# A different order for the S5 part of a hybrid backbone kernel: Toeplitz transfers, lag matrices, two sums and two pair steps

## The chip, the cores and the metric

The kernel runs on one core of one Trainium2 chip. A core has TensorE (PE in the profile; its weight loads are PEld), VectorE (DVE), ScalarE (ACT), GpSimd (POOL) and SyncE (SP, which here only issues DMAs). Time is device microseconds of one execution; lower is better.

## The reference, cut to what matters

With DEPTH = 1 the backbone is one layer: a bidirectional S5 mixer (64 groups of 16 channels, 64 complex states each) and a SwiGLU feed-forward part, both behind an RMS norm with a modulation (shift, scale, gate) that comes from the conditioning vector by one large matrix, `ada_w`. There are 1024 latent tokens of width 1024, and 256 context tokens that only feed the first state of each scan.

```python
m_l = jnp.split(sc @ ada_w[i] + ada_b[i], N_MOD, axis=-1)      # sc = silu(c), ada_w is 1024 x 6144
h_l = modulate(rms_norm(x, norm_mix[i]), m_l[0][:, None], m_l[1][:, None])
...
lam_bar = jnp.exp(lam * jnp.exp(log_step)[:, None])             # per direction
b_bar = ((lam_bar - 1.0) / lam)[..., None] * lax.complex(b_re, b_im)
bu = jnp.einsum('lgh,gnh->lgn', u, b_bar)
bu = bu.at[0].add(lam_bar * h0)                                 # h0: the context's last state
_, h = lax.associative_scan(_linear_combine, (a, bu), axis=0)
y = jnp.einsum('lgn,ghn->lgh', h, c_mat).real                   # forward plus backward
...
y = y.reshape(h.shape) + d_skip * h
g = jax.nn.gelu(y)
y_l = g * jax.nn.sigmoid(g @ w_glu + b_glu)
x = x + m_l[2][:, None] * y_l
h_l = modulate(rms_norm(x, norm_ffn[i]), m_l[3][:, None], m_l[4][:, None])
x = x + m_l[5][:, None] * swiglu(h_l, ffn_w1[i], ffn_w3[i], ffn_w2[i])
return rms_norm(x, norm_final)
```

## The kernel before, in words

The tokens are cut into chunks of 8. The scan runs over chunks only: 32 of the context, then 128 of the latents. What a token gets from tokens of its own chunk is a product with a Toeplitz matrix; what it gets from earlier chunks is the chunk's start state times factors. The 64 groups are worked in four quarters q of 16 groups (eight group pairs) and in 16 half-blocks `hb` (eight blocks of 8 groups, two directions).

*The first part* (a loop over `hb`) makes the chunk sums of each half-block on PE (`sums`), copies them to the state store `STQ` in SBUF, and joins neighbouring chunks there: `pair(hb, eng)` is four tensor-tensor instructions, on GpSimd for the half-blocks listed in `PPAIR` and on VectorE for the others; `pair(hb - 1, ...)` is issued in round `hb`, the last one, 15, behind the loop. The first tiles of the second part of `ada_w` are loaded here (`ADA2`).

*The scan* (`scan`) then runs on VectorE as one long chain of small instructions, with `fill_ops` between them. Meanwhile the other engines go through PROG1, a string of steps that `run` executes word by word. Each engine works its own share of these words in this order, so the string is at the same time the order of PE's, ACT's, POOL's and SP's queues. The steps that matter here:

- `A`n: modulation tiles up to number n (of 64). A tile is 128 x 512 of `ada_w`, 256 KB; `ada` multiplies it on PE (L534) into one PSUM bank `pm` and issues on SP, in `ada_load` (L523), each later tile whose buffer has been freed (`was`): tiles 42 to 45 reuse the buffers of 30 to 33, 46 to 49 those of 34 to 37, 50 to 53 those of 38 to 41, 54 to 57 those of 46 to 49, 58 to 61 those of 50 to 53, and 62 and 63 those of 54 and 55.
- `B`: the input factors are turned (L821). `O`: a PSUM bank is cleared on ACT for a `K` step.
- `C`qp: factors of quarter q, made on POOL by `cl_ops`. For each direction there are two products and a sum (parts 0 and 2, first half of the list), then a product and a sum (parts 1 and 3). `HOWS` says how each sum is made: `P` on PE with the unit matrix (four matmuls, L691) with two copies out by ACT (L692), `Y` by an accumulating DMA, `E` on POOL by one tensor-tensor instruction of 128 x 1024.
- `K`i: lag matrices of half a quarter (`k_mats`): many small matmuls (L839 to L847), two copies out on ACT and two DMAs that ACT issues to DRAM (L852). It needs both directions of the quarter's factors.
- `T`u: one Toeplitz transfer on SP (L860), 256 KB from DRAM to one of four buffers `KQ`; T0 to T3 need K0 and K1, T4 to T7 need K2 and K3, and so on.
- `L`, `G`, `q`: load of a quarter's output matrix (issued by ACT), its sign change on ACT (L669), its sum on POOL.
- `F`: a fill of a quarter's odd chunk states on POOL (eight instructions). F11 keeps temporaries where step R1 later writes.
- `R`i: the backward states of block i, turned by a copy on ACT (L954). `P`i: the block's output for the first half of the chunks on PE, a Toeplitz part (`x_mm`, L985, it needs T(2i) and T(2i+1)) and a state part (`states_mm`, L974, it needs R); `S` and `X` are the same two parts apart. `Y`: copies to SBUF on ACT (L1044).
- `M`: the finished modulation is copied (ACT), written to DRAM (SP, L933), transposed (PE, L937) and used.

After PROG1, PROG2 handles the second half of the chunks (`Z`, `N`, `D`), the GELU and the gated linear unit; `N0` is its first PE work. The feed-forward part follows, long streams of matmuls on PE.

PROG1 begins, before: `A22 G1 B0 A26 A30 C01 A34 A38 O0 C03 q1 A42 K0 A46 K1 L2 A50 C10 C11 A54 T0 T1 T2 T3 O2 C12 C13 G2 A58 K2 A64 K3 L3 F10 q2 C20 F11 R0 P0 ...`

Of the kernel before, what the change touches and what calls it, by code (L numbers as in the profile page):

```python
# [26 lines left out]
NS = 64  # L27
EPS = 1e-6
MAGIC = 12582912.0
HOWS = "YPYP EPEP PPPP EEEE"  # L30
ZEN = "VVSVSVSV"
PROG1 = ("A22 G1 B0 A26 A30 C01 A34 A38 O0 C03 q1 A42 K0 A46 K1 L2 A50 C10 C11 A54 T0 T1 T2 T3 O2 C12 C13 G2 A58 K2 A64 K3 L3 F10 q2 C20 F11 R0 P0 Y0 Y1 T4 T5 R1 P1 Y2 Y3 T6 T7 M0 M1 C22 G3 R2 P2 Y4 Y5 C21 R3 P3 Y6 Y7 C23 q3 K4 K5 T8 T9 T10 T11 C30 C31 C32 C33 R4 P4 Y8 Y9 R5 P5 Y10 Y11 O6 K7 K6 T12 T13 T14 T15 w0 l1 M2 m0 F31 w1 R6 S6 R7 S7 X6 Y12 Y13 X7 Y14 Y15")
PROG2 = ("Z0 N0 Z1 Z2 D0 Z3 N1 D1 Z4 H0 H1 N2 D2 Z5 H2 N3 D3 Z6 H3 N4 Z7 D4 H4 I0 J0 N5 D5 I1 J1 H5 W0 W1 N6 D6 I2 J2 H6 I3 J3 W2 W3 x0 x1 x2 x3 N7 D7 I4 J4 H7 V1 b0 w20 w21 l1 I5 J5 g03 g13 I6 J6 g23 g05 g15 I7 J7 V2 g26 x10 x11 x12 x13")
NS1, NS2 = 10, 1
LOG2E = 1.4426950408889634
# [7 lines left out]
def s5_ffn_kernel(tc, a, out):  # L43
    nc = tc.nc
    V, S, E, PE, SY = nc.vector, nc.scalar, nc.gpsimd, nc.tensor, nc.sync
    ctx = ExitStack()
    with ctx:
        ctx.enter_context(tc.manual_schedule())
        sb = ctx.enter_context(tc.tile_pool(name="sb", bufs=1))
        def region(tag, kb, dt=F32):  # L50
            return sb.tile([P, int(kb * 256)], dt, tag=tag, name=tag)
# [12 lines left out]
        R0 = region("r0", 7)  # L64
# [11 lines left out]
        def tt(o, x, y, op, eng=V):  # L76
            eng.tensor_tensor(out=o, in0=x, in1=y, op=op)  # L77
# [104 lines left out]
        def t_(i):  # L182
            return view(RA, 0.75 + 0.25 * i, [G])
# [11 lines left out]
        def ada1(h, *ks):  # L195
            for k in ks:
                for b in range(2):
                    i = 2 * b + h
                    PE.matmul(prow[32 * i:32 * i + 2], scs[:, k], stage[h][k][:, b], start=k == 0, stop=k == 7, tile_position=(0, 32 * i))
# [16 lines left out]
        k3, r1, pw2, be, al, rp, r2, u2, pw3, sn, q1, q2, tc_, td_ = [t_(i) for i in range(14)]  # L216
# [176 lines left out]
        def bd(hb):  # L393

            return divmod((0, 2, 1, 3)[hb] if hb < 4 else hb, 2)
# [63 lines left out]
        def mix_rows():  # L459
            S.copy(r4, prow.rearrange("p (m n) -> p m n", m=4))  # L460
# [38 lines left out]
        def u_act(b, n0, n1):  # L499
            for g in range(8 * b + n0, 8 * b + n1):  # L500
                S.activation(X[:, g], X[:, g], AF.Identity, bias=cols[:, 0, 0, g:g + 1], scale=cols[:, 0, 1, g:g + 1])
# [78 lines left out]
        def sums(hb):  # L580
            b, d = bd(hb)
            for j in range(2):
                w, pv = Win[hb % 3][:, j], pv2()
                for ri in range(2):
                    for i in range(4):
                        c0 = 160 * (i // 2)
                        PE.matmul(pv[64 * (i % 2):64 * (i % 2) + 64, ri, c0:c0 + 160], w[:, i, 64 * ri:64 * ri + 64],  # L587
                                  U[:, 8 * b + 4 * j + i], start=True, stop=True)
                pv = pv[:, :, 0:320].rearrange("p r (e c) -> p c r e", e=2)
                e = 8 * (b % 2) + 4 * d + 2 * j  # L590
                st = STQ[b // 2][:, :, :, e:e + 2]
                if d == 0:
                    S.copy(st, pv)
                else:
                    cp = V.tensor_copy if (hb, j) == (13, 1) else S.copy
                    cp(st[:, 159:31:-1], pv[:, 32:160])
                    cp(st[:, 31::-1], pv[:, 0:32])
# [10 lines left out]
        def rot(*args):  # L608
            for op in rot_ops(*args):
                op()  # L610

        def rots(*args):

            for a_ in args:
                rot(*a_, V, (LTb, lbt[:, 256:512]))
# [13 lines left out]
        def pair(hb, eng):  # L629
            b, d = bd(hb)  # L630
            e = 8 * (b % 2) + 4 * d
            st = STQ[b // 2][:, :, :, e:e + 4]
            a_ = (st[:, 33:96:2], st[:, 32:95:2], LQ[0] if eng is V else LS[:, 0], 16 * (b // 2) + e)
            if eng is V:
                rots(a_)
            else:
                rot(*a_, E, ptmp)
# [33 lines left out]
        def cs_sum(q):  # L671
            c0, c1, c2 = (Cs[q % 2][:, i].rearrange("p d g h -> p (d g h)") for i in range(3))
            tt(c2, c0, c1, SUB, E)
# [3 lines left out]
        def cl_ops(q, d):  # L677
# [5 lines left out]
            def prod(i, o):  # L683
                tt(o, bc(Cs[q % 2][:, (2, 1, 0)[i], d], 2, T), bc(fac[i][:, ::1 - 2 * d].rearrange("p t a -> p a t"), 3, HC), MUL, E)

            def add(o, how, last):
                if how == "P":
                    for h in range(2):
                        hs, pc = slice(4 * h, 4 * h + 4), pw([512])
                        for i, src in enumerate((o, ct)):  # L690
                            PE.matmul(pc, ident, src[:, hs].rearrange("p g t h -> p (g t h)"), start=i == 0, stop=i == 1)  # L691
                        S.activation(o[:, hs].rearrange("p g t h -> p (g t h)"), pc, AF.Copy, scale=-1.0 if last else 1.0)  # L692
                elif how == "Y":
                    E.dma_start(o, ct, accum_op=ADD)
                else:
                    tt(o, o, ct, SUB if last else ADD, E)

            h0, h1 = HOWS.split()[q][2 * d:2 * d + 2]
            return [lambda: prod(0, ct), lambda: prod(1, o0), lambda: add(o0, h0, False), lambda: prod(2, o1), lambda: add(o1, h1, True)]

        PPAIR = (3, 5, 7, 8, 9, 11, 12, 13, 15)
        UACT = {1: (2, 0, 4), 2: (2, 4, 8), 3: (3, 0, 4), 4: (3, 4, 8)}
        UACT.update({5 + i: (4 + i // 2, 4 * (i % 2), 4 * (i % 2) + 4) for i in range(8)})
        UCTX = {1: 2, 3: 3, 6: 4, 7: 5, 9: 6, 11: 7}
# [13 lines left out]
        for hb in range(16):  # L718
            sums(hb)
            ada1(1, *ADA1.get(hb, ()))  # L720
            if hb == 0:
                power8()
            if hb == 3:
                mix_rows()
            if hb >= 11 and hb in UACT:
                u_act(*UACT[hb])
            for n in BLTR.get(hb, (hb + 2,)):
                if n < 16:
                    bl_tr(n)
            if hb == 3:  # L730
                mix_turn()
            if hb == 4:
                mix_scale(1)
                mix_sel(1)
            if hb in RSL:
                rs_lat(RSL[hb])
            if hb == 4:
                mix_cols(1)
                tq = pA.tile([P, 512], F32, tag="r3", name="tq")
                LQ += [t[:, o_:o_ + 192].rearrange("p (r e) -> p r e", e=G) for t, o_ in ((tq, 0), (tq, 192), (LTb, 256))]  # L740
            if hb == 0:
                tt(Xc[:, 16:], ctxT[:, 16:], bc(rcp, 1, G - 16), MUL)
            if hb == 1:
                powers(0)
            if hb == 2:
                powers(1)
                SY.dma_start(BXY[:, 1], a["bxy"][:, 3])
                SY.dma_start(abr, a["abr"])
            if hb < 11 and hb in UACT:
                u_act(*UACT[hb])  # L750
            if hb in UCTX:
                u_ctx(UCTX[hb])
            if hb in (9, 10):
                bl_sum(hb + 5)
            if hb >= 1:
                pair(hb - 1, E if hb - 1 in PPAIR else V)
            if hb == 5:
                powers(2, 3)
            for a_ in CTREE.get(hb, ()):
                ctx_tree(*a_)  # L760
            if hb + 6 in (7, 9, 11, 12, 14, 15):
                lb_psum(hb + 6)
            if hb not in (9, 10):
                bl_sum(hb + 5)
            bl_make(hb + 6)
            if hb == 3:
                pw_mul(PW[:, 2:3], PW[:, 0:1], PW[:, 1])
                tt(KD.rearrange("p q g h -> p (q g) h"), bc(pat, 1, 8), bc(dcol, 2, HC), MUL, E)
            if hb == 4:
                pw_mul(PW[:, 4:6], PW[:, 0:2], PW[:, 3])  # L770
                pw_mul(PW[:, 6:7], PW[:, 2:3], PW[:, 3])
            if hb in (6, 8):
                pw_full(hb // 2 - 3)
            if hb == 6:
                cs_load(0)
            if hb == 8:
                cs_sign(0)
            if hb == 11:
                V.tensor_copy(LQ[4], SQ[4])
                cs_load(1)  # L780
            if hb == 12:
                cs_sum(0)
            for _ in range(CLAT.get(hb, 0)):
                CL0.pop(0)()
            ada_load(ADA2.get(hb, 0))
# [380 lines left out]

        run(PROG1)
        psW.__exit__(None, None, None)
# [160 lines left out]
        G2 = region("c3", 16, R32)  # L1329
# [503 lines left out]
```

## Time and profile before

| | us |
|---|---|
| median of 3 runs (lowest, highest) | 1036.97 (1035.01, 1037.14) |
| the profiled execution | 1037.25 |
| its span, first to last instruction | 1035.40 |
| busy in the span: PE, PEld, DVE | 972.2, 757.4, 782.9 |
| busy in the span: ACT, POOL | 434.7, 741.8 |
| mean granted PE clock (1 is full) | 0.983 |

Lines of the timeline read: start, duration, engine, source line, operation, written tile <- read tiles, size, count, and in brackets the idle time of the engine just before and what ended it. Rows for `SPq` and `ACTq` are issues of DMAs, not their transfers; where a DMA ended a wait, the brackets of the waiting engine say so. A row for a stretch of time gives each engine's busy time in it, with the number of instructions, then the granted clock, the busy share of the DMA engines and the GB/s that they moved. Rows of waits read: who waited, for whom, total, times, longest. Nearly all tensor-tensor instructions are issued through one helper, so they carry one line, L77; they are told apart by their tiles and times: `c` are the four 16 KB regions (factors, staging), `ra` holds the chunk states, `rxc` the output matrices, `rxa`, `rw`, `lta`, `ltb` and `r` small operands and temporaries, `kd` the lag matrices in DRAM, `kt`, `pw`, `pm` and `pe` PSUM banks.

### The profile page before, as it was taken

What the parts mean: (1) busy time and instruction counts of PE and PEld (TensorE: products, weight loads), DVE (VectorE), ACT (ScalarE), POOL (GpSimd) and SP (SyncE); (2) the same over time, 40 slices, a digit from 0 to 9 for tenths busy, and PEclk for the clock granted to TensorE, in tenths of its full rate; (3) what the DMA queues carried; (4) which work ended last, traced back from release to release, by engine and by line L of the source; (5) the groups of instructions that cost most, each with busy time, mean ns of one, the idle gap of its engine ahead of it and who ended that gap; (6) DMA issues with size and microseconds to landing.
All of it is one profiled execution on the core that took longest, in us unless ns stands there. A gap on an engine that the chain in (4) does not pass through costs nothing. (4 is left out here: it accounts for less than half of the span.)

```text
span 1035.4 us, 17785 instructions
## 1 busy us (share of the span) xinstructions
PE 972.2 (94%) x6628; PEld 757.4 (73%) x6628; DVE 782.9 (76%) x1642; ACT 434.7 (42%) x820; POOL 741.8 (72%) x582
## 2 busy tenths in 40 slices
PE   5987887978999999999999999999999999999996
PEld 1466422657878878787888888888888888888885
DVE  7979899980655687777976858685867768685977
ACT  4478421322643565433334342433334343424337
POOL 5799996390382455978787787868687877778673
PEclk9999998988999999999999999999999999999999
DMA  9765995223352003111211112121211121121204
GB/s 336 271 140 111 300 327 178 63 55 80 114 204 81 1 2 139 45 41 41 70 28 56 61 42 72 51 72 41 82 41 58 35 61 57 46 72 51 72 22 162
DMA packets 48542, 97.86 MB, mean 95 GB/s; under 512 B 4284, under 2 KB 18876, under 8 KB 47176
## 3 DMA queue, kind: packets, MB, share of 16 engines
q1 hardware_dynamic: 43416, 86.64, 25.3%
q0 software_dynamic: 2016, 7.34, 3.8%
q10 hardware_dynamic: 3024, 2.74, 0.9%
q8 instruction: 52, 0.85, 0.3%
q14 instruction: 34, 0.28, 0.1%
HBM read 83.20 MB, written 6.17 MB: 86 GB/s over the span
## 5 line engine op out<-in xcount | busy, mean ns | idle before, releaser
L77 POOL TENSOR_TENSOR c<-rxc,c 128x512 fp32r<-128x512 f32 x127 | 166.0, 1320 | 53.1 <-ACT c L1288 52.3
L1347 PE MATMUL ut<-ra,c 128*128 128x512 f32 x400 | 155.7, 389 | 1.2 <-DVE ra L77 1.2
L1346 PE MATMUL ut<-ra,c 128*128 128x512 f32 x400 | 155.7, 389 | 0.2 <-ACT ra L1288 0.2
L1348 PE MATMUL ut<-ra,c 128*128 128x512 f32 x400 | 155.6, 389 | 0.0
L1288 ACT CAST c<-rxc 128x512 fp32r<-128x512 f32 x128 | 79.1, 622 | 146.7 <-PE xt L1641 53.0
L1641 PE MATMUL xt<-c,c 128*128 128x512 f32 x540 | 129.7, 389 | 0.0
L77 DVE TENSOR_TENSOR ru<-ru,xt 128x1024 f32<-128x1024 f32 x90 | 107.9, 1217 | 13.4 <-PE xt L1641 9.4
L1641 PEld LDWEIGHTS xt<-c,c 128*128 128x128 f32 x540 | 101.4, 188 | 21.0
L77 DVE TENSOR_TENSOR ru<-ut,ru 128x512 f32<-128x512 f32 x98 | 67.2, 687 | 42.9 <-PE ut L1348 37.4
L1347 PEld LDWEIGHTS ut<-ra,c 128*128 128x128 f32 x400 | 75.1, 188 | 17.0 <-POOL rxc L77 1.5
L1346 PEld LDWEIGHTS ut<-ra,c 128*128 128x128 f32 x400 | 75.1, 188 | 16.2 <-ACT ra L1288 0.6
L1348 PEld LDWEIGHTS ut<-ra,c 128*128 128x128 f32 x400 | 75.1, 188 | 15.5
L77 POOL TENSOR_TENSOR rxc<-rxc 128x512 f32<-128x512 f32 (+1 forms) x44 | 64.6, 1469 | 24.2 <-ACT rxc L669 14.0
L77 POOL TENSOR_TENSOR c<-ru,c 128x512 fp32r<-128x512 f32 (+1 forms) x39 | 58.7, 1505 | 10.1 <-ACT c L1288 5.7
L77 POOL TENSOR_TENSOR c<-rw,c 128x512 fp32r<-128x512 f32 (+1 forms) x28 | 37.4, 1337 | 37.7 <-ACT c L1288 37.7
L1346 PE MATMUL ut<-c,c 128*128 128x512 f32 x160 | 62.3, 390 | 0.8 <-DVE rxa L77 0.8
L1348 PE MATMUL ut<-c,c 128*128 128x512 f32 x160 | 62.3, 389 | 0.0
L1347 PE MATMUL ut<-c,c 128*128 128x512 f32 x160 | 62.2, 389 | 0.0
L1641 PE MATMUL ut<-c,c 128*128 128x512 f32 x216 | 51.9, 389 | 0.0
L77 DVE TENSOR_TENSOR ru<-ru,ut 128x512 f32<-128x512 f32 x76 | 47.3, 681 | 0.3
L1641 PEld LDWEIGHTS ut<-c,c 128*128 128x128 f32 x216 | 40.6, 188 | 8.4
L587 PE MATMUL pv<-ru,c 128*64 128x160 f32 x512 | 40.8, 309 | 5.2 <-ACT c L450 2.0
(453 smaller groups left out, 2425.8 us busy)
## 6 DMA issues: line engine op xcount, KB each, us to landing
c<-in_ada_w SPq DMA_DIRECT2D x46, 256.0 KB
rxc<-in_w SPq DMA_DIRECT2D x38, 256.0 KB
rxc<-in_w SPq DMA_DIRECT2D x19, 512.0 KB
ru<-in_w SPq DMA_DIRECT2D x11, 512.0 KB
rw<-in_w SPq DMA_DIRECT2D x11, 512.0 KB
ra<-in_ada_w SPq DMA_DIRECT2D x10, 512.0 KB
c<-c POOLq DMA_DIRECT2D x9, 512.0 KB, 5.4
ra<-in_ada_w SPq DMA_DIRECT2D x18, 256.0 KB
```

What stands on the lines that cost most here:

```text
L77: eng.tensor_tensor(out=o, in0=x, in1=y, op=op)
L587: PE.matmul(pv[64 * (i % 2):64 * (i % 2) + 64, ri, c0:c0 + 160], w[:, i, 64 * ri:64 * ri + 64], U[:, 8 * b + 4 * j + i], start=True, stop= ...
L1288: S.copy(o[0], x)
L1346: PE.matmul(pu, wh, bh, start=start, stop=False)
L1347: PE.matmul(pu, wh, bl, start=False, stop=False)
L1348: PE.matmul(pu, wl, bh, start=False, stop=stop)
L1641: PE.matmul(pd, w[:, cs_], b, start=j in (1, 2, 4) and n == 0, stop=n == 2, skip_group_check=j not in (1, 2, 4))
```

## The change

Four things change, none of them in what is computed.

1. PROG1: T0 to T3 move behind A58, that is, behind the loads of the last modulation tiles in SP's order.
2. PROG1: C03 moves ahead of A34, K0 ahead of A38 and A42, K1 and C10, C11 ahead of A46; K2 comes ahead of G2 and A64; F10 and q2 come ahead of K3; M0 and M1 come ahead of T4; C30 and C31 come ahead of K5. POOL's own order stays as it was.
3. HOWS, third quarter: the first sum of each direction (in C20 and C22) is made on POOL instead of PE.
4. The pair step of half-block 12 goes to VectorE, one round sooner, and that of half-block 14 goes to GpSimd.

```diff
-HOWS = "YPYP EPEP PPPP EEEE"
+HOWS = "YPYP EPEP EPEP EEEE"
-PROG1 = ("A22 G1 B0 A26 A30 C01 A34 A38 O0 C03 q1 A42 K0 A46 K1 L2 A50 C10 C11 A54 T0 T1 T2 T3 O2 C12 C13 G2 A58 K2 A64 K3 L3 F10 q2 C20 F11 R0 P0 Y0 Y1 T4 T5 R1 P1 Y2 Y3 T6 T7 M0 M1 C22 G3 R2 P2 Y4 Y5 C21 R3 P3 Y6 Y7 C23 q3 K4 K5 T8 T9 T10 T11 C30 C31 C32 C33 R4 P4 ...")
+PROG1 = ("A22 G1 B0 A26 A30 C01 O0 C03 q1 A34 K0 A38 A42 K1 L2 C10 C11 A46 A50 O2 C12 C13 A54 A58 T0 T1 T2 T3 K2 G2 A64 F10 q2 K3 L3 C20 F11 R0 P0 Y0 Y1 M0 M1 T4 T5 R1 P1 Y2 Y3 T6 T7 C22 G3 R2 P2 Y4 Y5 C21 R3 P3 Y6 Y7 C23 q3 K4 C30 C31 K5 T8 T9 T10 T11 C32 C33 R4 P4 ...")
...
-        PPAIR = (3, 5, 7, 8, 9, 11, 12, 13, 15)
+        PPAIR = (3, 5, 7, 8, 9, 11, 13, 14, 15)
...
-            if hb >= 1:
+            if hb >= 1 and hb != 13:
                 pair(hb - 1, E if hb - 1 in PPAIR else V)
...
             if hb == 12:
+                pair(12, V)
                 cs_sum(0)
```

More of the change, by code (lines that the diff above doesn't have):

```diff
@@ L29 @@
 MAGIC = 12582912.0
-HOWS = "YPYP EPEP PPPP EEEE"
+HOWS = "YPYP EPEP EPEP EEEE"
 ZEN = "VVSVSVSV"
-PROG1 = ("A22 G1 B0 A26 A30 C01 A34 A38 O0 C03 q1 A42 K0 A46 K1 L2 A50 C10 C11 A54 T0 T1 T2 T3 O2 C12 C13 G2 A58 K2 A64 K3 L3 F10 q2 C20 F11 R0 P0 Y0 Y1 T4 T5 R1 P1 Y2 Y3 T6 T7 M0 M1 C22 G3 R2 P2 Y4 Y5 C21 R3 P3 Y6 Y7 C23 q3 K4 K5 T8 T9 T10 T11 C30 C31 C32 C33 R4 P4 Y8 Y9 R5 P5 Y10 Y11 O6 K7 K6 T12 T13 T14 T15 w0 l1 M2 m0 F31 w1 R6 S6 R7 S7 X6 Y12 Y13 X7 Y14 Y15")
+PROG1 = ("A22 G1 B0 A26 A30 C01 O0 C03 q1 A34 K0 A38 A42 K1 L2 C10 C11 A46 A50 O2 C12 C13 A54 A58 T0 T1 T2 T3 K2 G2 A64 F10 q2 K3 L3 C20 F11 R0 P0 Y0 Y1 M0 M1 T4 T5 R1 P1 Y2 Y3 T6 T7 C22 G3 R2 P2 Y4 Y5 C21 R3 P3 Y6 Y7 C23 q3 K4 C30 C31 K5 T8 T9 T10 T11 C32 C33 R4 P4 Y8 Y9 R5 P5 Y10 Y11 O6 K7 K6 T12 T13 T14 T15 w0 l1 M2 m0 F31 w1 R6 S6 R7 S7 X6 Y12 Y13 X7 Y14 Y15")
 PROG2 = ("Z0 N0 Z1 Z2 D0 Z3 N1 D1 Z4 H0 H1 N2 D2 Z5 H2 N3 D3 Z6 H3 N4 Z7 D4 H4 I0 J0 N5 D5 I1 J1 H5 W0 W1 N6 D6 I2 J2 H6 I3 J3 W2 W3 x0 x1 x2 x3 N7 D7 I4 J4 H7 V1 b0 w20 w21 l1 I5 J5 g03 g13 I6 J6 g23 g05 g15 I7 J7 V2 g26 x10 x11 x12 x13")
```

## The prediction

> **What bounds the kernel now.** I read the page's busy shares first, then the busy time of each engine in five stretches, cut where the named steps of the program begin, then who waited for whom.
>
> ```profile
> PE 972.2 (94%) x6628; PEld 757.4 (73%) x6628; DVE 782.9 (76%) x1642; ACT 434.7 (42%) x820; POOL 741.8 (72%) x582
> 120.00:138.00 18.00, 16.68 (x85) 2.74 (x78) 17.62 (x92) 2.86 (x6) 17.25 (x15) 1.00 1.02 322
> 138.00:180.66 42.66, 34.92 (x532) 12.31 (x533) 42.66 (x244) 8.49 (x19) 33.36 (x29) 0.89 0.76 250
> 180.66:204.59 23.93, 22.03 (x405) 17.19 (x404) 23.93 (x138) 7.85 (x17) 9.83 (x6) 0.99 0.26 68
> 204.59:261.28 56.69, 44.32 (x994) 35.93 (x992) 23.33 (x105) 14.08 (x30) 25.66 (x20) 0.85 0.29 76
> 261.28:1035.40 774.12, 761.43 (x3845) 630.52 (x3844) 571.35 (x769) 322.91 (x590) 557.11 (x406) 1.00 0.19 63
> DVE ru L77 <- PE pe L974: 37.5, 5, 35.7
> ```
>
> Behind the time and the length of a stretch stand PE, PEld, DVE, ACT and POOL, then the granted clock and the DMA share. From 261.28 on PE works 761.43 of 774.12 us: that part is PE's, and it starts when PE has gone through PROG1. The scan on DVE is done long before (last row: DVE waits 35.7 us for the first late states), so before 261.28 PE's own queue, in program order, sets the end, and what it loses there comes 1:1 into the time. Between 138 and 261.28 it is idle 22 us. All edits lie there or just ahead.
>
> **Where PE's queue stands.** Step names are those of PROG1; four modulation tiles are one A step of 4.
>
> ```profile
> 136.94 1.02 PE L534 MATMUL pm<-c,r 128*2 128x512 f32 x2 [0.26 <-DMA c<-in_ada_w]
> 145.52 3.70 PE L691 MATMUL pw<-c,r 128*128 128x512 f32 x8
> 149.15 1.04 PE L534 MATMUL pm<-c,r 128*2 128x512 f32 x8
> 151.73 1.04 PE L534 MATMUL pm<-c,r 128*2 128x512 f32 x8
> 168.22 1.04 PE L534 MATMUL pm<-ra,r 128*2 128x512 f32 x8
> 171.32 1.03 PE L534 MATMUL pm<-c,r 128*2 128x512 f32 x6
> 177.27 1.87 PE L534 MATMUL pm<-c,r 128*2 128x512 f32 x2 [4.91 <-DMA c<-in_ada_w]
> 178.44 2.29 PE L534 MATMUL pm<-ra,r 128*2 128x512 f32 x4
> 196.59 0.66 PE L937 MATMUL pw<-r,ra 128*128 128x128 f32 x4 [1.64 <-ACT ra L931]
> 204.59 3.70 PE L691 MATMUL pw<-c,r 128*128 128x512 f32 x8
> 208.13 1.95 PE L985 MATMUL pw<-ra,ru 128*128 128x128 f32 x16
> 212.21 3.70 PE L691 MATMUL pw<-c,r 128*128 128x512 f32 x8
> 230.08 3.98 PE L985 MATMUL pw<-ra,ru 128*128 128x128 f32 x16 [2.40 <-DMA ra<-kd]
> 261.28 10.72 PE L974 MATMUL pe<-c,ra 64*64 64x128 f32 x320
> ```
>
> Prices from it. A sum done on PE ("P", L691): 3.70. Four tiles: 1.04. A lag-matrix step K lies between the end at 150.19 and 151.73: 1.5; K2, with waits, from 169.26 to 171.32: 2.1; I take 2.0. A P step (both its halves): 212.21 less the end of the sum before it (204.59 + 3.70), 3.9 to 4.1; its x part is 1.95, so the states part is 2.1.
>
> **The four edits.**
>
> *First Toeplitz transfers behind the last tiles.* SP issues in its own order:
>
> ```profile
> 164.67 1.28 SPq L523 DMA_DIRECT2D c<-in_ada_w  x3
> 166.05 4.96 SPq L860 DMA_DIRECT2D ra<-kd  x4
> 171.11 1.38 SPq L523 DMA_DIRECT2D c<-in_ada_w  x1
> 225.30 4.35 SPq L860 DMA_DIRECT2D ra<-kd  x4
> ```
>
> T0 to T3 (4.96) go out ahead of the last three tiles, tile 61 leaves at 171.11 and PE has it at 177.27: a wait of 4.91, and the tiles behind it run slowly (2.29 for two). With T0 behind A58 the tiles leave as soon as A54 and A58 free their buffers. T0 to T3 then have the tiles ahead of them. What is late next: P0 wants T0 and T1. A Toeplitz transfer needs 4.8 us from issue to use (225.30 to 230.08), which I also use as the longest a tile can take; 0.65 a tile is the other end (below).
>
> *First lag matrices sooner.* K0 moves ahead of A38 and A42, C03 ahead of A34, K1 ahead of A46. The work is the same; but A34 to A42 now come later, so the buffers for tiles 42 to 53 come free later. In the profile these steps waited for tiles anyway:
>
> ```profile
> 143.94 0.09 PEld L534 LDWEIGHTS pm<-ra,r 128*2 128x2 f32 x2 [0.52 <-DMA ra<-in_ada_w]
> 144.57 0.09 PEld L534 LDWEIGHTS pm<-ra,r 128*2 128x2 f32 x2 [0.54 <-DMA ra<-in_ada_w]
> ```
>
> 0.65 us a tile is the pace of the loads. Work put ahead of tiles that have not landed fills that wait, so I book no loss, and a gain of what the waits were. If the cover fails, each round trip from a freed buffer to a landed tile costs up to 4.8.
>
> *Two sums to POOL* (HOWS, third quarter, "PPPP" to "EPEP"). C20 and C22 lose a sum on PE, 3.70 and 3.60 (with 2 evictions on ACT each), and POOL gains two tensor-tensor instructions of 128x1024. POOL's order stays otherwise:
>
> ```profile
> 169.31 0.74 POOL L77 TENSOR_TENSOR rxc<-rxc 128x256 f32<-128x256 f32 x1 [8.68 <-PE pm L534]
> 170.12 2.03 POOL L77 TENSOR_TENSOR c<-rxc,rxa 128x1024 f32<-128x1024 f32 x1
> ...
> 174.07 1.40 POOL L77 TENSOR_TENSOR c<-ra,r 128x256 f32<-128x256 f32 x2
> ...
> 178.27 1.54 POOL L77 TENSOR_TENSOR ra<-ra,c 128x256 f32<-128x256 f32 x2
> ...
> 183.71 4.01 POOL L77 TENSOR_TENSOR c<-rxc,rxa 128x1024 f32<-128x1024 f32 x2
> ...
> 210.48 2.39 POOL L77 TENSOR_TENSOR c<-c,ra 128x1024 f32<-128x1024 f32 x1
> 168.82 0.41 ACT L669 ACTIVATE rxc<-rxc 128x256 f32<-128x256 f32 x1
> 171.49 0.36 ACT L851 COPY r<-kt 128x240 f32<-128x240 f32 x1 [2.26 <-PE pw L847]
> 172.64 0.33 ACTq L852 DMA_DIRECT2D kd<-r  x1
> ```
>
> In order: q2's sum (it starts when ACT's sign change at 168.82, G2, is done), C20's two products, the fill F11 (8 instructions, 174.07 to 179.81), C22's products, one product each for C21 and C23. The 2.39 row is the price of one sum on POOL: 4.8 for two. Behind C20's sum on POOL stands F11, behind F11 the R1 copy, which writes where F11 keeps temporaries, and P1; behind C22's sum stands C21's product, which PE's sum in C21 needs. These are the new waits.
>
> *Pair steps exchanged.* Step 12 goes from POOL to DVE, step 14 from DVE to POOL: on DVE four instructions of 0.42 leave (118.82 to 120.27) and four come, before the sums of half-block 13 are copied.
>
> ```profile
> 118.82 0.42 DVE L77 TENSOR_TENSOR ltb<-ra,lta 128x256 f32<-128x256 f32 x1
> 119.93 0.42 DVE L77 TENSOR_TENSOR ra<-ra,lbt 128x256 f32<-128x256 f32 x1
> ```
>
> The scan starts at most 1.5 earlier or 1.5 later. DVE's slack of 35.7 covers it, and PE waits for tiles then (136.94): zero, both ends far under the other terms.
>
> **The sum.** PE reaches the end of A30 at 137.96 in both, as tile 29's landing sets it. From there, in the new order: C01 and C03 7.4, A34 1.04, K0 2.0, A38 and A42 2.1, K1 2.0, C11 3.7, A46 and A50 2.1, C13 3.7, A54 and A58 2.1: 26.1, to 164.1 (169.26 before; the 5.2 are waits and slow-clock stretches now filled). K2 to 166.1. ACT then copies out and issues (171.49 to 172.97: 1.5) and does G2 (0.41): 168.0. So q2's sum on POOL starts 1.3 sooner, though K2 now stands ahead of G2. F11 ends at 179.8 - 1.3 + 2.4 = 180.9; C21's product, which ended at 185.7, now ends at 185.7 - 1.3 + 4.8 = 189.2.
>
> PE meanwhile: A64's tiles 58 to 61 left about 163, 62 and 63 by 164.7; by the two ends the last lands between 166 and 169.5, I take 168.5 (nearer the 4.8, as several tiles go together), so K3 ends at 170.5 (182.6 before). R0, behind K3's 1.5 on ACT, the L3 issue 0.7 and its own 0.6, is there at 173.3; P0 ends at 175.4. M0 and M1 come next (Y0 and Y1 1.1, copy 0.6, PE 0.66): 178. P1's x part to 180, its states behind R1 (180.9 + 0.6) to 183.6. SP sends M0's two writes ahead of T4 and T5, so these leave near 177.5 to 179 and are there by 183.8; P2 ends about 188. C21's sum therefore waits for POOL until 189.3, against 204.59 before: 15.3 sooner. From C21 on (P3, C23, K4 and K5, P4 to X7) order and waits are unchanged. R4 waits behind K5 on ACT, T8 to T11 behind K4 and K5, T12 to T15 behind K6, so they move along, and POOL's last products too. The first late states start at 246.0 instead of 261.28, when the scan has been done for some 20 us. All after it moves by the same 15.3.
>
> The profiled execution took 1037.25 (span 1035.40 and 1.85 around it): 1021.95. The median of the runs is 1036.97, 0.3 below it: 1021.7.
>
> **The rivals.**
> 1. *PE's front end is late.* Either a tile's round trip shows, 4.8 each, or P1 and P2 run at a low clock. What that costs is seen in the x parts of 208.13 and 230.08, 1.95 and 3.98, and in the clock of their stretches (1.00 and 0.50, third column from the right):
>
> ```profile
> 208.00:212.00 4.00, 4.00 (x81) 3.75 (x79) 4.00 (x25) 1.10 (x2) 3.54 (x2) 1.00 0.02 4
> 228.00:232.00 4.00, 1.92 (x9) 1.80 (x9) 0.43 (x1) 0.00 (x0) 3.84 (x9) 0.50 0.62 150
> ```
>
> P1 and P2 at half clock take 8.2 more, less the 1.3 that P2 has in hand and the 1.5 that P1 waits for R1: 5.4, so 1027.1; one round trip 1026.5; both at most 1030. For it: tiles 42 to 63 pass through the same buffers in several generations. Against: no wait that I see ahead of P2 exceeds 2.5 us.
> 2. *More is gained.* The wait of 2.40 at 230.08 goes and its x part runs at 1.95: 4.4 more, 1017.3. For it: nothing but a luckier fall of the same transfers.
> 3. *It doesn't do what it says*: the stall goes from the tiles to P0, which then waits for T1. If T1 came only when tile 62 does now (178.44), P0 would end at 182.5, P1 (0.66 for M1 ahead of it) at 187.3, P2 at 191.4, and C21 start then: 1023.8. Even so no zero.
> 4. *Slower*: the reload of a freed buffer becomes the pace. Four groups (42, 46, 50 and 54) are reloaded behind A34 and ahead of K2; exposed at 4.8 each they put K2 19.2 later, G2 and POOL's queue with its two new sums behind it, and C21 at 208.5: 1040.9. It decides from three groups on (14.4 of the 15.3 gone). Against it: the DMA share of 0.76 in 138 to 180.66 says that the loads have room, and C11, C13 and K1 lie between a freed buffer and its use.
>
> By the Trainium skill (TensorE: Matmul & The Clock Gate, section HAM oscillation) PE's clock is halved after gaps of more than about 3.4 us. The trace agrees: behind the wait of 4.91 the two tiles at 178.44 took 2.29. By that rule the low clock of rival 1 needs P0, M1 and P1 to wait in one piece, and would give 1027.
>
> **How the numbers follow.** Likeliest (POOL sets C21, the rest moves along): 0.5; its own range is 1019.5 (K at 1.5 instead of 2.0 each, and PE not waiting for POOL) to 1024. Rival 1: 0.2. Rival 2: 0.08. Rival 3: 0.1. Gain lost elsewhere, within 0.2% (2 us, about what a measurement of this kernel can tell): 0.05. Rival 4: 0.07. The range, 1017 to 1030, leaves the last two out. Faster 0.88, same 0.05, slower 0.07.
>
> **What would show it.** Six sums on PE at L691 instead of eight (8 records each). No PE wait of 4.9 for the last tiles; the first four Toeplitz issues behind the last tile. C20's and C22's products each followed by a POOL sum near 2.4. C21's sum on PE near 189, behind POOL. The first late states near 246 and DVE's wait for them near 21. Wrong if K2 is later than about 168, if P2 ends after 191, or if the distance from C21's sum to the first late states differs from 56.7.

## The result and the profile after

The changed kernel takes 1022.84 us (median of 4 runs, 1019.46 to 1023.28) against 1036.59 us of the kernel before on the same chip: a ratio of 0.9863, 95% interval 0.9839 to 0.9887. Beside a second set of runs it gave 0.9873 (0.9844 to 0.9903). The profiled execution took 1023.28 us, with a span of 1021.50; before it was 1037.25 and 1035.40. In the changed file the lines behind the diff's new line 782 are numbered one higher (L974 is L975, L860 is L861, L985 is L986).

Of the page, the busy time of each engine; PE has 16 records less (two sums of 8), POOL two more:

```profile
PE 961.0 (94%) x6612; PEld 755.5 (74%) x6612; DVE 778.3 (76%) x1642; ACT 432.8 (42%) x816; POOL 746.9 (73%) x584
```

The five stretches, cut at the same steps as before: time and length, busy time and count of PE, PEld, DVE, ACT and POOL, granted clock, DMA share, GB/s. (The fourth is cut half a microsecond ahead of the first late states, which have their row below.)

```profile
120.00:138.00 18.00, 15.57 (x87) 3.35 (x88) 17.33 (x91) 3.62 (x9) 17.17 (x17) 0.91 1.00 325
138.00:171.46 33.46, 31.04 (x532) 11.97 (x530) 33.46 (x192) 8.40 (x19) 26.57 (x21) 1.00 0.91 292
171.46:190.38 18.92, 15.25 (x389) 13.94 (x388) 18.92 (x109) 5.68 (x13) 18.61 (x15) 1.00 0.48 133
190.38:246.85 56.47, 45.03 (x993) 36.55 (x992) 34.53 (x186) 13.97 (x29) 29.65 (x23) 0.81 0.29 78
246.85:1021.50 774.65, 762.07 (x3847) 630.95 (x3846) 569.83 (x769) 322.98 (x590) 557.84 (x406) 1.00 0.19 63
```

The gain lies in the second and third rows alone. Up to the end of the last modulation tiles the stretch fell from 42.66 to 33.46 with the same 532 PE records: PE's idle time in it went from 7.7 to 2.4, and the clock from 0.89 to 1.00. From there to C21's sum it fell from 23.93 to 18.92, less than the 7.30 that the two sums took on PE, because PE's idle time in it rose from 1.9 to 3.7. Behind C21's sum nothing changed: 57.0 to the first late states (190.39 to 247.38), and 774.1 from these to the end, as before. In all fourteen profiles of this text the stretch from the first late states to the end takes 773.2 to 774.2, so what moves these moves the time.

PE's own rows, to set beside those of before; what an instruction waited for stands in brackets:

```profile
136.96 1.12 PE L691 MATMUL pw<-c,r 128*128 128x512 f32 x2 [1.61 <-POOL c L77]
...
166.21 1.21 PE L534 MATMUL pm<-c,r 128*2 128x512 f32 x4
168.43 1.68 PE L534 MATMUL pm<-c,r 128*2 128x512 f32 x4 [1.02 <-DMA c<-in_ada_w]
169.84 1.69 PE L534 MATMUL pm<-ra,r 128*2 128x512 f32 x4
...
175.01 1.16 PE L986 MATMUL pw<-ra,ru 128*128 128x128 f32 x8 [0.64 <-DMA ra<-kd]
180.00 0.66 PE L938 MATMUL pw<-r,ra 128*128 128x128 f32 x4 [1.64 <-ACT ra L932]
...
185.29 1.13 PE L986 MATMUL pw<-ra,ru 128*128 128x128 f32 x8 [0.65 <-DMA ra<-kd]
187.10 1.16 PE L986 MATMUL pw<-ra,ru 128*128 128x128 f32 x8 [0.68 <-DMA ra<-kd]
190.39 3.70 PE L691 MATMUL pw<-c,r 128*128 128x512 f32 x8
...
247.38 10.79 PE L975 MATMUL pe<-c,ra 64*64 64x128 f32 x320
```

The wait of 4.91 for the last tiles has become one of 1.02; more waiting lies inside the slow rows, since A64's six tiles took 5.3 from 166.21 to 171.53 (before, 9.4 from 171.32 to 180.73) where four tiles in a row take 1.04. What came in its place are waits of 0.64 to 0.68 for Toeplitz transfers, one in P0 and two in P2. C21's sum (190.39) stands behind no wait. The first row is new: C01 waits 1.61 for its product on POOL.

SP's queue, with the transfers now behind the last tiles:

```profile
164.48 0.86 SPq L523 DMA_DIRECT2D ra<-in_ada_w  x2
165.39 8.07 SPq L861 DMA_DIRECT2D ra<-kd  x4
179.97 0.56 SPq L934 DMA_DIRECT2D mbd<-ra  x2
180.71 34.88 SPq L861 DMA_DIRECT2D ra<-kd  x8
```

Tile 63 leaves near 165.3 and lands at 170.46, and PE has done with it at 171.53. T0 to T3 take 8.07 to issue where they took 4.96.

POOL's queue, and DVE's wait for the first late states:

```profile
168.59 0.73 POOL L77 TENSOR_TENSOR rxc<-rxc 128x256 f32<-128x256 f32 x1 [6.42 <-ACT rxc L669]
173.47 2.36 POOL L77 TENSOR_TENSOR c<-c,c 128x1024 f32<-128x1024 f32 x1
...
180.02 1.55 POOL L77 TENSOR_TENSOR ra<-ra,c 128x256 f32<-128x256 f32 x2
...
185.62 2.36 POOL L77 TENSOR_TENSOR c<-c,c 128x1024 f32<-128x1024 f32 x1
187.94 4.01 POOL L77 TENSOR_TENSOR c<-rxc,rxa 128x1024 f32<-128x1024 f32 x2
250.26 1.29 DVE L77 TENSOR_TENSOR ru<-pe,ru 128x512 f32<-128x512 f32 x2 [24.84 <-PE pe L975]
```

The two new sums are the rows of 2.36. F11 ends at 181.57; C21's product is the first of the two at 187.94 and ends at 189.95. So POOL was ready 0.4 ahead of C21's sum on PE.

### The profile page after: what moved, and what is told of

It is laid out like the page before. It is cut to its first block, busy times and chain, and to the rows that moved or that the text cites. A ratio compares the mean times of both kernels' runs of the same rounds, so it can differ in the third digit from the quotient of the medians.

```text
span 1021.5 us, 17745 instructions
## 1 busy us (share of the span) xinstructions
PE 961.0 (94%) x6612; PEld 755.5 (74%) x6612; DVE 778.3 (76%) x1642; ACT 432.8 (42%) x816; POOL 746.9 (73%) x584
## 5 line engine op out<-in xcount | busy, mean ns | idle before, releaser
L77 DVE TENSOR_TENSOR pe<-pe,ru 128x512 f32<-128x512 f32 x32 | 22.3, 696 | 30.8 <-PE pe L1165 16.3
## 6 DMA issues: line engine op xcount, KB each, us to landing
ra<-in_ada_w SPq DMA_DIRECT2D x10, 512.0 KB, 10.8
```

## The experiments

Ratios are to the kernel before on the same chip, with their 95% intervals. All edits but two are in the order PROG1 or in HOWS; only the steps that differ are shown.

### Taking one edit out of the changed kernel

`a_no_t`: T0 to T3 go ahead of A58 again, all else as changed.

```diff
-A54 A58 T0 T1 T2 T3 K2
+A54 T0 T1 T2 T3 A58 K2
```

> The changed kernel with T0 to T3 ahead of A58 again, so that the loads of tiles 61 to 63 stand behind them on SP; the rest of the change stays. Theory 1 (this order made the old wait of 4.9): tile 61 leaves near 168 and lands near 174.5, A64 ends near 177 instead of 171.5; P0 doesn't wait for T1 then, so 4 to 5 us come back: 1026.5 to 1028, with a PE wait of 4 to 6 for a modulation tile. Theory 2 (the wait was made by the late A steps, not by SP's order; with them sooner SP has time): no PE wait over 2, 1022 to 1024.

Measured: 1028.38 us, 0.9932 (0.9914 to 0.9949), so 0.7% of 1036 is the price of this order. The first theory holds; the time and the wait lie a little above its ranges. SP and PE of this kernel:

```profile
163.37 4.68 SPq L861 DMA_DIRECT2D ra<-kd  x4
168.16 1.39 SPq L523 DMA_DIRECT2D c<-in_ada_w  x1
...
174.29 1.01 PE L534 MATMUL pm<-c,r 128*2 128x512 f32 x1 [7.01 <-DMA c<-in_ada_w]
196.93 3.70 PE L691 MATMUL pw<-c,r 128*128 128x512 f32 x8
```

Tile 61 again leaves behind them, at 168.16, and PE waits 7.01 for it, more than the 4.91 of before: with the lag matrices done sooner PE comes to the last tiles earlier and finds the same late tile. C21's sum is 6.5 later than in the changed kernel, and the first late states (253.24) are 5.9 later.

`a_no_sums`: HOWS as before, all else as changed.

```diff
-HOWS = "YPYP EPEP EPEP EEEE"
+HOWS = "YPYP EPEP PPPP EEEE"
```

> The changed kernel with C20's and C22's sums back on PE (HOWS third quarter PPPP); the rest of the change stays. Theory 1 (PE's queue up to C21 sets the time, and what PE gains by the two sums is time): C20's sum lies between K3 and P0, where PE now waits 0.6 for T1, C22's between P1 and P2, where it waits 1.3 for T4 and T5. So of 7.4 us on PE about 4.5 to 6 come back: 1027 to 1029, PE's sum in C21 near 195 instead of 190.4. Theory 2 (POOL's queue sets the start of C21 anyway, the two sums only moved from one queue to the other): POOL is 4.8 earlier, PE 7.4 later, result within 2 us of the changed kernel, 1021 to 1025.

Measured: 1027.09 us, 0.9925 (0.9908 to 0.9942). PE of this kernel:

```profile
174.55 5.40 PE L691 MATMUL pw<-c,r 128*128 128x512 f32 x8 [1.07 <-POOL c L77]
190.13 3.70 PE L691 MATMUL pw<-c,r 128*128 128x512 f32 x8
197.75 3.70 PE L691 MATMUL pw<-c,r 128*128 128x512 f32 x8
```

C20's sum back on PE waits 1.07 for POOL's product and runs 5.40, not 3.70: the granted clock was 0.50 from 176 to 178. C21's sum comes at 197.75, some 2.7 later than the 195 worked out beforehand. The two sums do fill waits, as the first theory said: those of 0.64 in P0 and of 0.65 and 0.68 in P2 are gone here. But C20's sum costs 2.8 more than its 3.70, so C21's sum still stands 7.36 behind that of the changed kernel. Moving the sums was worth 0.62%; that the time fell into the expected 1027 to 1029 is in part luck.

`a_no_pair`: the pair steps as before, all else as changed.

```diff
-PPAIR = (3, 5, 7, 8, 9, 11, 13, 14, 15)
+PPAIR = (3, 5, 7, 8, 9, 11, 12, 13, 15)
-            if hb >= 1 and hb != 13:
+            if hb >= 1:
-                pair(12, V)
```

> The changed kernel with the pair steps as before (12 on GpSimd in its old round, 14 on VectorE). In the changed kernel's trace the scan starts at 125.52 as before (125.49) and POOL's third-quarter chain waits for G2, so nothing hangs on it: within 2 us of the changed kernel, 0.985 to 0.988 of the time before. Rival (the exchange carries part of the gain, since the last pair steps release POOL's factors and PE's first sums): 2 us or more slower, above 0.989.

Measured: 1021.63 us, 0.9875 (0.9843 to 0.9907): not to be told from the changed kernel. The exchange is worth nothing that these runs can show, as booked. One row of it matters below: here C21's sum did wait for POOL, by 0.41.

```profile
190.86 3.70 PE L691 MATMUL pw<-c,r 128*128 128x512 f32 x8 [0.41 <-POOL c L77]
```

### Making one edit alone in the kernel before

`b_t`: T0 to T3 behind A58, the rest of the old order kept.

```diff
-A54 T0 T1 T2 T3 O2 C12 C13 G2 A58 K2
+A54 O2 C12 C13 G2 A58 T0 T1 T2 T3 K2
```

> The kernel before with one part of the change alone: T0 to T3 behind A58. The wait of 4.9 for tile 61 and the slow two tiles behind it (1.2) go; everything from K3 on moves along, as C20's products on POOL (done at 174.1) and F11 (179.8) are early enough. Theory (SP's order made the wait): 5 to 6.5 gained, 0.9940 to 0.9950 of the time before. Rival (the wait moves to P0, which lacks T0 and T1): less than 2 gained, above 0.998.

Measured: 1031.02 us, 0.9952 (0.9935 to 0.9968). That is just outside the theory's range, and the interval leaves out the rival's 0.998. The profiled execution, at 1035.65, was the slowest of ten, and shows where a gain can be lost again:

```profile
173.85 1.39 PE L534 MATMUL pm<-ra,r 128*2 128x512 f32 x4
178.71 0.17 PE L847 MATMUL pw<-rxc,c 64*16 64x16 f32 x1 [2.26 <-issue]
179.20 5.40 PE L691 MATMUL pw<-c,r 128*128 128x512 f32 x8
202.92 3.70 PE L691 MATMUL pw<-c,r 128*128 128x512 f32 x8
```

The wait of 4.91 is gone, and the last tile is done 5.5 sooner than before (175.24 for 180.73). Then K3 stands still for 2.26, for which the profile shows no cause, C20's sum runs 5.40 (the granted clock was 0.50 from 180 to 182), and C21's sum is only 1.7 sooner (202.92 for 204.59). What the faster executions kept of the gain is not seen in it.

`b_sums`: HOWS as changed, the old order kept.

```diff
-HOWS = "YPYP EPEP PPPP EEEE"
+HOWS = "YPYP EPEP EPEP EEEE"
```

> The kernel before with the two sums of the third quarter on POOL alone. PE loses 3.7 between K3 and P0 and 3.6 between M1 and P2; POOL's product for C21 ends 4.8 later, at 190.5, PE comes to C21 at about 197.3. Theory 1 (PE's queue carries the time): 6 to 7.4 gained, 0.9930 to 0.9942. Theory 2 (the work only changes its queue; PE then waits for POOL or for F11): under 3 gained, above 0.997.

Measured: 1029.53 us, 0.9937 (0.9912 to 0.9962), inside the first theory's range. PE came to C21's sum at 197.19, where 197.3 was expected.

`b_k`: C03, K0, K1 and C11 sooner, T0 to T3 still ahead of A58.

```diff
-A30 C01 A34 A38 O0 C03 q1 A42 K0 A46 K1 L2 A50 C10 C11 A54 T0
+A30 C01 O0 C03 q1 A34 K0 A38 A42 K1 L2 C10 C11 A46 A50 A54 T0
```

> The kernel before with the lag matrices, C03 and C11 sooner among the A steps as in the change, but T0 to T3 still ahead of A58, and sums and pair steps as before. Theory (C03, K0, K1 and C11 fill the waits for tiles, 5.2 by A58): A58 ends near 163.5 instead of 169.3; tile 61 stands behind T0 to T3 as before, so the wait stays at 5 to 6, but all of it sooner: 5 to 6.5 gained, 0.994 to 0.995. Rival (the old wait absorbs it: tile 61 lands no sooner, as T0 to T3 then wait longer): under 2 gained, above 0.998.

Measured: 1034.65 us, 0.9980 (0.9960 to 1.0000). The main theory missed: it wanted 0.994 to 0.995. The time is the rival's, at the edge of its 0.998, and the trace shows how. SP and PE of this kernel:

```profile
162.31 7.10 SPq L860 DMA_DIRECT2D ra<-kd  x4
169.52 1.35 SPq L523 DMA_DIRECT2D c<-in_ada_w  x1
...
176.30 1.01 PE L534 MATMUL pm<-c,r 128*2 128x512 f32 x1 [6.29 <-DMA c<-in_ada_w]
202.89 3.70 PE L691 MATMUL pw<-c,r 128*128 128x512 f32 x8
```

T0 to T3 go out sooner (162.31 for 166.05), but they take 7.10 to issue and not 4.96, so tile 61 leaves only 1.6 sooner (169.52 for 171.11). Part of what PE gained in front of the tiles turned into wait: 6.29 instead of 4.91. But the gain in front was small too: A58 ended at 167.35, 1.9 sooner than before, where 163.5 was expected. So the theory failed twice, in what the sooner steps fill and in what then waits; why A58 came no sooner was not tried.

The three gains alone, 0.48%, 0.63% and 0.20%, add to 1.31%; all together gave 1.37% and 1.27%. Within the intervals they add. The transfers are worth 0.48% alone and 0.69% when taken out of the changed kernel; the intervals are too wide to show this difference by the times. The traces point that way: with the transfers in their old place PE waits 4.91 and 5.01 (`b_sums`) for tile 61 in the old order of the lag matrices, 6.29 and 7.01 in the new one. The order of the lag matrices was not taken out of the changed kernel, and the other moves of the second edit (K2, F10 and q2, M0 and M1, C30 and C31) were not run alone.

### What held C21's sum: POOL, or PE's own P1 and P2

`a_g2`: G2, and with it q2's sum on POOL, sooner.

```diff
-C13 A54 A58 T0 T1 T2 T3 K2 G2 A64
+C13 G2 A54 A58 T0 T1 T2 T3 K2 A64
```

> The changed kernel with one more edit: G2, the sign change that POOL's sum q2 waits for, ahead of A54, so that it no longer stands behind K2's copies on ACT. POOL's part of the third quarter starts near 162.5 instead of 168.6, 6 us sooner. Theory 1 of the prediction (POOL sets the start of C21): C21 is then held by PE alone, 190.4 becomes what P2's end allows. In the changed kernel's trace P2 ends at 190.4 too, held by T4 and T5, so by the trace: 0 to 0.6 us gained, 1022 to 1023.5. If POOL were what held PE: 2 us or more gained, below 1021.

Measured: 1022.76 us, 0.9880 (0.9857 to 0.9902): no gain over the changed kernel. POOL and PE of this kernel:

```profile
161.07 0.73 POOL L77 TENSOR_TENSOR rxc<-rxc 128x256 f32<-128x256 f32 x1
...
178.32 0.66 PE L938 MATMUL pw<-r,ra 128*128 128x128 f32 x4 [1.65 <-ACT ra L932]
183.58 1.13 PE L986 MATMUL pw<-ra,ru 128*128 128x128 f32 x8 [0.61 <-DMA ra<-kd]
185.54 1.16 PE L986 MATMUL pw<-ra,ru 128*128 128x128 f32 x8 [0.83 <-DMA ra<-kd]
188.83 3.70 PE L691 MATMUL pw<-c,r 128*128 128x512 f32 x8
```

POOL starts 7.5 sooner (161.07 for 168.59), and F11 and all products move with it. C21's sum moves by 1.6 only, about as far as M1 does (178.32 for 180.00), and M1 moved as the last tiles were done 2.1 sooner in that execution (169.45 for 171.53). From M1 to C21's sum it takes 10.5 with POOL early and 10.4 with POOL as it is; the waits for T4 and T5 stand in both. In the changed kernel P1 and P2 held C21's sum at least as long as POOL did.

`a_g2_e4`: `a_g2`, and all four sums of the third quarter on POOL. It leaves out the change of sign that the second factors need for that, which in `best` only divides the work of two GpSimd instructions otherwise (16 to 16 instead of 24 to 8).

```diff
-HOWS = "YPYP EPEP EPEP EEEE"
+HOWS = "YPYP EPEP EEEE EEEE"
```

> As the last one, and with all four sums of the third quarter on POOL (HOWS EEEE): C21's and C23's sums leave PE too, 7.4 us, and POOL, which starts 6 us sooner, takes them for 4.8. Theory 1 (PE's queue carries the time, POOL has room once G2 is early): K4 near 194.5 instead of 201.6, 7 us gained, 1015 to 1017. Theory 2 (POOL becomes the bound): its last sum ends later than PE's P3, K4 waits, and less than 3 us are gained, 1020 to 1023.

Measured: 1017.33 us (median of 5), 0.9841 (0.9816 to 0.9866), a little above the first theory's range. With G2 early POOL has room for two more sums. K4 starts near 193.7 (201.6 in the changed kernel), the first late states at 240.10.

### Going on from there

Four kernels on one chip: the changed one again (`after_again`), and three that build on the last experiment with its sign put right.

`best`:

```diff
-HOWS = "YPYP EPEP EPEP EEEE"
+HOWS = "YPYP EPEP EEEE EEEE"
-C13 A54 A58 T0 T1 T2 T3 K2 G2 A64
+C13 G2 A54 A58 T0 T1 T2 T3 K2 A64
-            b3, b2 = slice(24, 32), slice(0, 24)
+            b3, b2 = slice(16, 32), slice(0, 16)
```

`best3` and `best2` add to it:

```diff
 best3
-R0 P0 Y0 Y1 M0 M1 T4 T5 R1 P1
+R0 P0 Y0 Y1 T4 T5 M0 M1 R1 P1
 best2
-R0 P0 Y0 Y1 M0 M1 T4 T5 R1 P1 ... R3 P3 Y6 Y7 C23 q3
+R0 P0 Y0 Y1 T4 T5 R1 P1 ... R3 P3 M0 Y6 Y7 M1 C23 q3
```

> The changed kernel once more, beside the kernels that go on from it, on one chip. Its ratio to the kernel before was 0.9863; expected 0.985 to 0.989. The terms found so far alone (Toeplitz transfers 0.48%, two sums 0.63%, order of the lag matrices 0.20%, pair steps nothing) add to 1.31%, so a ratio of 0.987 would say that they simply add.

> The changed kernel with G2 right behind C13 (K2 behind it) and both other sums of the third quarter on POOL too (HOWS EPEP EPEP EEEE EEEE, with the second factors' sign to suit). Theory 'PE's queue ahead of the late states is the bound, and POOL has room once G2 is early': two more sums of 3.7 leave PE, one behind C21 (full gain) and one in C23, so that the late states start near 240 and not 247: 6 to 7 us less than the changed kernel, about 1016, ratio 0.981 to 0.985. Rival 'POOL becomes the bound': the four sums in a row on POOL put K4 behind C23's last sum, and the gain stays under 3 us, 1020 (ratio 0.985 to 0.987).

> As the kernel labelled best, with the Toeplitz transfers T4 and T5 issued ahead of M0 and M1 and not behind them. It tells what held P2 and so C21 in the changed kernel: by the theory 'M0's two writes on SP put T5 late' the wait of P2's second half goes and the late states start 0.7 to 1.7 us sooner than in best, about 0.999 of its time; by the rival 'the pace of PE's own work and of POOL's fill F11 holds P1, and P2 with it' they start within 0.4 us of those of best, and the time is the same within 0.1%.

> As the kernel labelled best, with M0 behind P3 and M1 behind Y7: T4 and T5 go out sooner still and M0's copy and M1's wait leave the way of P1 and P2. Theory 'PE's waits and small steps ahead of C21 come 1:1 into the time': M1's 0.66 and its wait of 1.6 leave that place, and C21, C23 and K4 come 1.5 to 2.5 us sooner, 0.9980 of best. Rival 'POOL's last sum of C23 (ending near 189.7) holds K4': K4 comes at most 2 us sooner whatever PE gains, and the time falls by 0 to 2 us; a later M0 (whose result the second half of the program reads) costs nothing unless its readers now wait.

| kernel | us, median of 6 | ratio to before | K4 starts | first late states | between | clock between |
|---|---|---|---|---|---|---|
| after_again | 1022.18 | 0.9873 (0.9844 to 0.9903) | 201.30 | 247.26 | 45.96 | 0.81 |
| best | 1017.51 | 0.9826 (0.9795 to 0.9857) | 194.52 | 242.76 | 48.24 | 0.75 |
| best3 | 1014.94 | 0.9803 (0.9776 to 0.9830) | 194.25 | 243.29 | 49.04 | 0.73 |
| best2 | 1014.80 | 0.9795 (0.9767 to 0.9822) | 193.38 | 238.03 | 44.65 | 0.81 |

`best2` is faster than both the kernel before and the changed one: its interval lies clear of that of the changed kernel. Against `best` it is not shown: K4 comes 1.1 sooner, less than its theory wanted (1.5 to 2.5) and within its rival's 0 to 2; the rest of the 4.7 at the first late states lies behind K4, and the intervals overlap. In `best` POOL does not become the bound: its last sum for C23 is this row, and ends at 190.27, 4.2 ahead of K4.

```profile
187.89 2.38 POOL L77 TENSOR_TENSOR c<-c,c 128x1024 f32<-128x1024 f32 x1
```

`best3` against `best` is inconclusive. M1 and the two halves of P2, in `best`:

```profile
179.44 0.66 PE L938 MATMUL pw<-r,ra 128*128 128x128 f32 x4 [1.64 <-ACT ra L932]
184.71 1.13 PE L986 MATMUL pw<-ra,ru 128*128 128x128 f32 x8 [0.63 <-DMA ra<-kd]
186.56 1.16 PE L986 MATMUL pw<-ra,ru 128*128 128x128 f32 x8 [0.71 <-DMA ra<-kd]
```

and M1 in `best3`, which has no wait for a transfer behind it up to K4:

```profile
180.28 0.66 PE L938 MATMUL pw<-r,ra 128*128 128x128 f32 x4 [1.64 <-ACT ra L932]
```

From M1 to K4 it takes 13.97 instead of 15.08, so T4 and T5 were late by what the waits say. But M1 was 0.84 later in that execution, and the first late states came no sooner (243.29 for 242.76), while the median says 2.6 us less, with intervals that overlap. Both theories can't be told apart by this.

The last two columns, the time from K4 to the first late states and the mean granted clock in it, say why a microsecond or two is hard to show. The order from K4 to the first late states is the same in all four, yet it took 44.65 to 49.04, and the two longest have the lowest mean granted clock. In the changed kernel the granted clock falls to half in the middle of it; time and length, busy times, clock, DMA share, GB/s:

```profile
208.00:210.00 2.00, 0.20 (x4) 0.01 (x1) 2.00 (x13) 0.56 (x2) 2.00 (x2) 1.00 0.22 68
212.00:214.00 2.00, 1.93 (x33) 1.53 (x26) 2.00 (x13) 0.00 (x0) 1.95 (x1) 0.50 0.26 69
214.00:216.00 2.00, 0.03 (x1) 0.04 (x1) 2.00 (x13) 0.00 (x0) 1.92 (x6) 0.50 0.60 136
222.00:224.00 2.00, 2.00 (x48) 2.00 (x44) 1.86 (x9) 0.00 (x0) 0.00 (x0) 0.50 0.00 0
```

PE is almost idle from 208 to 210 and again from 214 to 216; full work from 216 on still has half the clock at 224. Idle time of PE in this stretch seems to be paid twice, by itself and by the slow clock behind it; that the one brings the other is read from the order of the rows and was not tried. Single executions are wider apart than such edits, too: the six of `a_g2` lie between 1019.54 and 1026.80. Which edit would keep the clock up from K4 on was not tried.

## Why the prediction was right, point by point

The forecast of 1021.7 (median) and 1021.95 (profiled execution) came out at 1022.84 and 1023.28: 1.1 and 1.3 late, inside the likeliest case's own range.

- *The bound.* Right. PE in program order ahead of the first late states sets the end, and what is taken away there comes 1:1 into the time. C21's sum came 14.2 sooner (204.59 to 190.39), the first late states 13.9 (261.28 to 247.38), the span 13.9. The distance between the two was booked as 56.7 and was 57.0; so close a fit is partly luck, since the eight other profiles with C21's sum on PE show 55.2 to 57.2.
- *PE up to K2.* Right in the total, with errors that partly cancel: 164.1 and 166.1 forecast; A58 ended near 164.7 and ACT's copy of K2's result starts at 166.57. A30 was booked to end at 137.96 in both kernels; it ended at 135.3, C01 waited 1.61 for POOL, and the sum's first step started 1.0 early, at 136.96. From there to A58's end it took 27.7, not 26.1: K1 took 3.4 (booked 2.0), and A54 with A58 3.2 (booked 2.1). Of the 5.2 of waits and slow clock that were to be filled, 4.6 were; the clock of the stretch is 1.00 now. No reload of a freed buffer showed as an idle time over 1.02, so the rival that ended slower had no ground.
- *The last tiles.* The step that was sized wrong. I had the end of A64 at 168.5 and the latest end at 169.5; it was 171.53. Tiles 62 and 63 left as forecast (164.7, in fact 164.48 to 165.34), but tile 63 took 5.5 from issue (164.95) to landing (170.46), and its product on PE, for which nothing was booked, about 1. The sum had 3.8 and allowed 4.8 at most. That 4.8 was a Toeplitz transfer's, at 225 to 230, where the DMA share was 0.62. A nearer row stood in the same profile: tile 61 of the kernel before, issued at 171.11 and in use at 177.27, took 6.2. Here the share is 0.91 over the whole stretch, and tiles and T0 to T3 are under way together. That the shared engines made the tiles slow is argued from these rows and was not tried alone. The term is too small in every execution: in the nine profiles with the new order of the lag matrices and T0 to T3 behind A58, A64 ends at 169.4 to 171.5. K3, P0 and M1 followed 2.6 to 3.0 late, and P2 2.5.
- *C21's sum waits for POOL.* Wrong as a cause, small in size. POOL came as forecast: q2's sum at 168.59 (168.0), F11's end 181.57 (180.9), C21's product 189.95 (189.2), a sum on POOL 2.36 (2.4). But P2, forecast to end at 188, ended near 190.4, with the tiles' delay and waits for T4 and T5 in it, and `a_g2` shows that POOL's head start of 7.5 is worth nothing there. PE's own work and POOL arrived within half a microsecond of one another (in `a_no_pair` POOL came last, by 0.41), so the same sum came out by another last arrival. That the start of C21's sum is off by 1.1 and not by P2's 2.5 is luck: the forecast had POOL, 1.3 behind P2, in that place. To start POOL sooner pays only with two more sums moved to it, as `a_g2_e4` and `best` show.
- *The Toeplitz transfers late for P0.* The third rival was right in kind: P0's second half waited for T1, but by 0.64 and not by 5. The first rival's two costs, 5.4 and 4.8, add to 1031.9 and not to "at most 1030"; neither came.
- *Pair steps.* Zero, as booked, but not untouched: with the exchange C01 waits 1.61 for POOL and starts at 136.96; without it (`a_no_pair`) it waits for nothing, but A30 ends at 136.75 and C01 starts at 136.68. The first late states' wait on DVE is 24.84 where I wrote about 21: the scan was done by 225 either way, and the wait shrank by 10.8, not by the whole 13.9, since the wait of before had been cut by slow copies (below).

The Trainium skill (TensorE: Matmul & The Clock Gate, section HAM oscillation) was drawn on for a low clock in P1 and P2. The trace has none there: the clock is 1.00 from 171.46 to 190.38, and no wait of PE in that stretch is over 1.64. But the gap of 3.4 that the Trainium skill gives there does not decide it here. From K4 on the clock does halve, as the rows above show, though PE's longest wait up to then is 2.47; and in `a_no_sums` it was 0.50 under C20's sum, behind waits of 0.93 and 1.07.

## What to carry to other kernels

When one engine runs a written order, price each edit as what that engine loses or fills, then ask which two arrivals meet at the next join: if they come within a microsecond of each other, moving one of them sooner pays nothing until the other moves too. A transfer queued ahead of the last loads costs more the sooner the engine comes to them, so part of what is gained before the late load turns into wait (4.91 became 6.29 in `b_k`), and the load's place in the queue is mended first. Price a transfer that shares the queue with others in flight by rows where it does, not by a row where it is alone.

## What was not expected of the hardware

The copies of turned states on DVE, which neither kernel changes. Before, and then the two POOL instructions at that time, then after:

```profile
224.64 3.79 DVE L956 COPY ra<-ra 128x512 f32<-128x512 f32 x2
223.63 2.03 POOL L77 TENSOR_TENSOR c<-rxc,rxa 128x1024 f32<-128x1024 f32 x1
225.74 2.41 POOL L77 TENSOR_TENSOR c<-c,rw 128x1024 f32<-128x1024 f32 x1
```

```profile
224.66 0.76 DVE L957 COPY ra<-ra 128x512 f32<-128x512 f32 x2
```

With POOL idle (after: its last instruction ended at 220.7) two copies take 0.76; with POOL at work they take 3.79 and end at 228.43, 0.3 behind the end of the second POOL instruction (228.15). The scan's tensor-tensors, one operand of which lies in PSUM, take 0.29 in both. The Trainium skill (SBUF — State Buffer, section SBUF: two separate sides) says that DVE in a two-port mode and GpSimd share a port pair by an exclusive lock, held for the whole instruction; the trace agrees, since each copy ended 0.28 behind a POOL instruction that ran when it began. It cost nothing here, as DVE then waits over 20 us for PE. That these copies run in a two-port mode is not shown by the trace, and that the lock is the cause was not tested by a run of its own.

The other surprise was the issue time of the same four Toeplitz transfers on SP: 4.96 before, 4.68 in `a_no_t`, 7.10 in `b_k`, 8.07 in the changed kernel, each time right behind tile loads on that queue. What sets it stays open. It cost nothing that shows where only T4 stood behind; in `b_k`, where tile 61 stood behind, T0 left 3.7 sooner and tile 61 only 1.6.
